# High and low parts of 109 weight units made by a rounding and an adding DMA on GpSimd's queue instead of ScalarE and VectorE

## The chip, the cores and the metric

The kernel runs on one core of a Trainium2 chip. The metric is the device time of one execution in microseconds. Before the change two runs gave 855.59 and 856.32 us, median 855.96 us.

The engines are called by their names in the profile: PE is TensorE's matrix multiplication and PEld its loading of weights, DVE is VectorE, ACT is ScalarE, POOL is GpSimd, SP is SyncE, which here only issues DMAs.

## The reference: what is computed

Two layers of a decoder trunk over 512 tokens of 1024 channels, in float32:

```python
for l in range(DEPTH):                                   # 2
    mod = c_act @ w_ada[l] + b_ada[l]
    shift, scale, gate = jnp.split(mod, 3, axis=-1)
    h = rms_norm(x, norm_g[l]) * (1.0 + scale[:, None, :]) + shift[:, None, :]
    u = h @ w_in[l]                                      # 1024 x 5120
    rg_x, rg_z, ml_x, ml_o, ml_z = jnp.split(u, split_pts, axis=-1)
    y_rg = rglru(causal_depthwise_conv(rg_x, ...), ...) * jax.nn.silu(rg_z)
    y_ml = mlstm_branch(ml_x, ml_o, ...) * jax.nn.silu(ml_z)
    y = jnp.concatenate([y_rg, y_ml], axis=-1) @ w_out[l]  # 2048 x 1024
    x = x + gate[:, None, :] * y
return rms_norm(x, final_g)
```

Most of the work lies in the two large products, `h @ w_in` and `y @ w_out`. The rest are the small block-diagonal products, the convolutions, the scan of the RG-LRU and the mLSTM's scores, gates and norms.

## The kernel before, in words

**Three products for one.** TensorE multiplies in the type `float32r`, which holds fewer bits than float32. To keep precision, every operand is split into a high part `hi`, the value rounded to float32r, and a low part `lo`, the rounded remainder, so that value = hi + lo nearly. `mm3` (L495) then issues three matrix multiplications for one: hi by hi, hi by lo and lo by hi.

**Weight units.** The weights are cut into units of 512 KB, tiles of 128 partitions by 1024 values. `load_raw` (L479) takes a tile of kind `raw` and has SP load it; `load_w` (L486) takes a tile `whi` and a tile `wlo` and splits the raw unit: ScalarE copies raw to hi (the copy rounds), VectorE subtracts hi from raw into lo. `split` (L464) is these two instructions. There are 3 raw slots, 4 slots `whi` and 4 slots `wlo` (L438 to L440). Three units of the front of layer 0, the first half of the rows of w_in for three groups of columns, are loaded and split in four pieces each (`pieces=4`, L1203).

The units go to these products, by the names that the profile uses for their output: `mx` (the mLSTM's input, `w_in_unit`, L724), `rgx` and `rgz` (through `chan_group`, L735), `oz` (the mLSTM's output gate and z, `ml_oz`, L959), `out` (first half of the output channels, `out_first`, L1116), and `outq` (third quarter in `out_quarter`, L1131; last quarter in `out_last`, L1146, whose four units are loaded at L1309 and held over four token blocks). Other loads stay with SP and with `split` or use raw tiles directly: `w_qk`, `w_vT`, `w_v`, `w_rg`, the adaLN weights `wada` and `w_ada2` (32 units through the raw slots, `mod_units`, L632), x, and small parameters.

**The stages of a layer.** The front computes shift, scale and h in five stages of channel blocks (layer 0: `STAGES`, L1190, with matrix products of the adaLN weights, `modps`, between them) and multiplies h with the first units of `mx`. Then come the per-head products (A, p, v, S), the gate chain (`gate_chain`, L906, with a power on GpSimd, the tile `u`), the four heads of oz with the mLSTM's tail (`num`, then `mrs`, a power on GpSimd, and the transposes `yT`), the RG-LRU half (rgx, gates, rgz, scan), and the output projection. In layer 0 the block norms of the next layer (`norm_x`, with `rstd`, a power on GpSimd) and the transposes `hT` start while the last quarter is still computed.

**What sets the order.** `Planner` (L108) records every instruction with a cost, its tiles and its engine, and then plans them all: `deadlines` (L243) goes backwards from TensorE's order and gives each instruction the latest time at which it must start, with 2.5 us on top for a DMA of SP; `schedule` (L286) plays the program forward, and at each moment an idle engine takes, of the instructions that are ready, the one with the earliest deadline. An engine doesn't idle if anything is ready. A tile gets a slot of its kind only if enough slots remain for tiles wanted earlier (`fits`, L313). The DMA engines are modelled as one server of 360 GB/s in order of issue, and a DMA of SP lands 2.0 us after that (L349 to L352). The result is a fixed order per engine, in which each engine works and waits on semaphores.

Of the kernel before, what the change touches and what calls it, by code (L numbers as in the profile page):

```python
# [13 lines left out]
F32R = mybir.dt.float32r  # L14
# [5 lines left out]
L = 2  # L20
# [10 lines left out]
# columns of the packed per-channel parameters  # L31
# [3 lines left out]
# what of adaLN is summed up on the vector engine: (layer, third)  # L35
# [3 lines left out]
# order of the rows of w_out: the mLSTM half first  # L39
CORD = list(range(8, 16)) + list(range(0, 8))  # L40
# where block j of the causal scores lies: (tile, first column)
# [4 lines left out]
class View:  # L46
    """A part of a logical tile; becomes an access pattern when its instruction is issued."""
# [60 lines left out]
class Planner:  # L108
    """Records instructions, then issues them on each engine in the order of a list schedule: the tensor
    engine follows the traced order, the others serve what it needs first."""  # L110
# [125 lines left out]

    def lat(self, a, b):
        if a != b:
            return self.LAT
        return 0.13 if a in ("DVE", "ACT", "POOL") else 0.0  # L240

# [1 line left out]
    def deadlines(self):  # L243
# [14 lines left out]
        # a PSUM bank is wanted again by a later tile; ready a little ahead of that  # L258
# [13 lines left out]
        for o in reversed(ops):  # L272
            d = o.pos
            for j in o.succ:
                s = ops[j]
                lat = self.lat(o.eng, s.eng)
                if o.eng == "SP":
                    lat += 2.5
                d = min(d, s.late - lat - o.cost)
            if o.eng != "PE":  # L280
                for b in o.tiles:
                    if b in after:
                        d = min(d, ops[after[b]].pos - o.cost)
            o.late = -100.0 if o.first else d

    def schedule(self):  # L286
# [4 lines left out]
        ready = {e: [] for e in engines}     # (late, i)  # L291
        events = []                          # (time, i): a finished instruction
        nfree = {k: [(0.0, s) for s in range(n)] for k, (n, _) in self.kinds.items()}
        # tiles still without a slot, by the deadline of their first use
# [18 lines left out]
        def fits(o):  # L313
            need = {}
            for b in o.tiles:
                if b.kind in self.kinds and b.slot is None:
                    need.setdefault(b.kind, []).append(b)
            for k, bs in need.items():
                room = len(nfree[k]) - len(bs)
                if room < 0:  # L320
                    return False
                # slots stay for the tiles that come before these
                ahead, w, h, last = 0, want[k], head[k], max(b.first for b in bs)
                while h < len(w) and w[h][0] < last:
                    if w[h][1].slot is None and w[h][1] not in bs:
                        ahead += 1
                        if ahead > room:
                            return False
                    h += 1
            return True  # L330

        def bank_free(o):
            # engines take turns at a PSUM bank
            return max((b.busy[1] for b in o.tiles if b.kind == "ps" and b.busy[0] != o.eng), default=0.0)

        def start(o, now):
# [12 lines left out]
            if o.eng == "SP":  # L349
                s = max(end, dma_free)  # L350
                dma_free = s + o.tail / 360e3
                end = dma_free + 2.0  # L352
# [5 lines left out]
        while done < len(ops):  # L358
# [23 lines left out]
            # next time at which something changes  # L382
# [43 lines left out]
def trunk_kernel(ctx: ExitStack, tc: tile.TileContext, x, cT, params, bif, bgate, fg,  # L426
# [6 lines left out]
    def pools(name, n, **kw):  # L433
# [5 lines left out]
        "whi": pools("whi", 4),  # L439
        "wlo": pools("wlo", 4),  # L440
# [53 lines left out]

    def mm3(ps, lh, ll, rh, rl, start, stop):  # L495
# [11 lines left out]
    # t < s: above any maximum, so that its exponential is 0; elsewhere below any  # L507
# [3 lines left out]
    # rows 32 q of four row groups; and pairs of groups, or all, row by row  # L511
# [42 lines left out]
    def log1p_exp_neg(ab, shape):  # L554
        # log(1 + exp(-ab)) for ab >= 0: u = exp(-ab), 2 atanh(u / (2 + u))
# [23 lines left out]
    # 4 softplus(-lambda), and halves of the biases of the RG-LRU gates, for both layers  # L579
# [18 lines left out]
    def mod_first(d0, nd):  # L598
        # shift and scale of the first layer, channel blocks d0 .. d0 + nd
# [5 lines left out]
        for k in range(4):  # L605
            # quadrants: (which, half of the rows)
# [25 lines left out]
    def mod_units(l, w):  # L632
        # third w (shift, scale, gate) of layer l: products and sums over the blocks of rows, one step a block
# [11 lines left out]
    def mod_sum(l, w):  # L645
        # the sum over the rows of a block
# [56 lines left out]
    def h_part(l, hT, xn, d0, nd, half):  # L703
        # channel blocks d0 .. d0 + nd of two token blocks, transposed, scaled, shifted, split
# [19 lines left out]
    def w_in_unit(l, g, kh, pieces=1):  # L724
        return load_w(w_in[l, g, kh], (4, 256), None, pieces)
# [27 lines left out]
    def silu2(ps, name, shape=(128, 512)):  # L753
        # 2 silu
# [15 lines left out]
    def fold(ps, sel, n):  # L770
        # rows 32 q + g of ps, transposed and summed over the groups q that sel joins: [128, chunk, n]
# [9 lines left out]
    def qk_weights(l, p, st):  # L781
        # A = w_q w_k^T, and the gates' weights seen through w_q and w_k
# [29 lines left out]
    def v_weights(l, u, st):  # L812
        # w_v of two heads, with the gates' columns beside it
# [24 lines left out]
    def ml_head(l, p, st):  # L838
# [34 lines left out]
        # scores, transposed, times 16; the gates' columns follow the last token  # L873
# [32 lines left out]
    def gate_chain(l, st):  # L906
# [13 lines left out]
        # sums of log f inside the blocks, and the blocks' totals on every partition  # L920
# [4 lines left out]
        # a[i - j][:, j]: log i - b of block j, from where block i starts  # L925
# [33 lines left out]
    def ml_oz(l, h, hT, st):  # L959
        # tanh(o / 2) and 2 silu(z) of a head, in two steps  # L960
        ps = [bank("oz") for _ in range(NB)]
        for u in range(4):
            wh, wl = load_w(w_oz[l, h, u], (2, 512))
# [16 lines left out]
    def ml_sw(h, st):  # L980
        # S * exp(a_s - M_t), causal, split
# [76 lines left out]
    def rg_gates(l, g, st):  # L1058
# [4 lines left out]
        for cc in range(2):  # L1063
# [6 lines left out]
            # r2 = 2 sigmoid(p) = (1 + |tanh(p / 2)|) exp(min(p, 0)); s = -log a = 4 sp r2;  # L1070
            # 1 - a^2 = tanh(s) (1 + a^2)
# [36 lines left out]
    def out_evac(l, ps, xt, cs):  # L1108
        # x + gate * y
# [6 lines left out]
    def out_first(l, st, xt, side):  # L1116
        y = st["y"]
        ps = [bank("out") for _ in range(NB)]
        for u in range(8):
            wh, wl = load_w(w_out[l, u], (2, 512))  # L1120
# [10 lines left out]
    def out_quarter(l, st, xt, side):  # L1131
        y = st["y"]
        ps = [bank("outq", (128, 256)) for b in range(NB)]
        for u in range(4):
            wh, wl = load_w(w_out[l, 8 + u], (4, 256))
# [20 lines left out]
    def final_pre(xt):  # L1156
        # of the first 768 channels: squares summed, x times the final gain
# [34 lines left out]
    for l in range(L):  # L1192
# [14 lines left out]
        if l == 0:  # L1207
            def front(n):
                # a stage's shift and scale, then its part of h, between the products of the stage before
# [99 lines left out]
        units = [load_w(w_out[l, 12 + u], (4, 256)) for u in range(4)]  # L1309
# [20 lines left out]
def _pack(inp):  # L1330
# [5 lines left out]
    def chan(v):  # [L, n * 128] -> [L, 128, n]  # L1336
# [7 lines left out]
    # adaLN, first layer's shift and scale: [channel block, k', p, quadrant, 128]; quadrant = (which, half of the rows)  # L1344
    wa = a["w_ada"].reshape(L, 2, 4, 128, 3, 8, 128)[0, :, :, :, 0:2]  # kh, k', p, which, block, n
    wa = wa.transpose(4, 1, 2, 3, 0, 5)  # block, k', p, which, half, n
# [4 lines left out]
    # o and z of a head side by side  # L1351
    oz = a["w_in"][:, :, 3072:].reshape(L, 4, 2, 128, 2, 4, 256)  # l, k pair, k, p, which, head, n
    w_oz = oz.transpose(0, 5, 1, 3, 2, 4, 6).reshape(L, 4, 4, 128, 1024)
    # transposed heads: l, h, m, e, d
# [7 lines left out]
    rg = np.stack([a["rg_w_a"], a["rg_w_x"]], axis=2)  # l, h, m, d, e  # L1362
# [32 lines left out]
```

## Time and profile before

| | |
|---|---|
| median of the runs | 855.96 us (855.59 to 856.32) |
| span of the profiled execution, first to last instruction | 853.5 us |
| granted TensorE clock, mean | 0.998 of full speed |
| DMA bytes moved | 107.60 MB, mean 126 GB/s |

The page gives no other time of the profiled execution than its span; 855.96 - 853.5 = 2.5 us lie around it, taken with the median of the runs.

How to read the profile. A group's row gives the source line, the engine, the operation, the output and input tiles with their shapes, the count, the busy time in us and the mean in ns, then the idle time of the engine just before the group's instructions and what ended it. In the view of waits a row says which engine and tile waited for which, the sum, the count and the longest. The chain is followed back from the last instruction, at each step to what released it. In the view of windows each row gives the stretch, its length, the busy time of PE, PEld, DVE, ACT and POOL with their counts, the granted clock, the share of the DMA engines' time and the GB/s. In the view of one tile, durations are minimum, median and maximum in ns. In the timeline a row starts with the start and the duration in us; SPq is the issue of a DMA by SP. Matrix multiplications are pipelined, so the durations of single ones overlap, and the chain shows their real pace.

### The profile page before, as it was taken

To read this page: it belongs to the slowest core of one execution; us is meant where nothing else is said; L and a number is where in the kernel's file an instruction comes from. 1 tells how busy PE (TensorE), PEld (TensorE's weight loads), DVE (VectorE), ACT (ScalarE), POOL (GpSimd) and SP (SyncE) were. 2 spreads that over 40 slices of the span, in tenths; PEclk is the share of its full clock that TensorE was granted. 3 is DMA by queue.
4 is the path that set the end of the run, shared out by engine and by line. 5 is a ranking of instruction groups with operands and counts; after the bars stand their busy time and mean duration, and the time that the engine had idled before them with its cause. 6 is when DMAs were issued, how large, how long until landed. Compare 5 with 4: busy or idle time off the path is not lost.

```text
span 853.5 us, 12548 instructions
## 1 busy us (share of the span) xinstructions
PE 835.0 (98%) x4664; PEld 698.1 (82%) x4664; DVE 607.3 (71%) x1227; ACT 476.7 (56%) x938; POOL 40.9 (5%) x66
## 2 busy tenths in 40 slices
PE   4999999999999999999999999999999999999996
PEld 3677897888888888887999789878888888888896
DVE  5467976898889699654466897376775877967643
ACT  4357763655457969622146766364454696893322
POOL 3000001011100000000010000100000000000000
PEclk9999999999999999999999999999999999999999
DMA  9924132466553323523231422033333222273202
GB/s 323 323 81 137 62 121 78 149 202 210 183 195 111 112 74 125 196 99 123 88 107 62 159 87 99 26 111 136 125 109 122 91 77 96 70 252 123 74 26 99
DMA packets 37053, 107.60 MB, mean 126 GB/s; under 512 B 4352, under 2 KB 6400, under 8 KB 36992
## 3 DMA queue, kind: packets, MB, share of 16 engines
q1 hardware_dynamic: 36992, 106.80, 36.2%
q8 instruction: 37, 0.61, 0.3%
q14 instruction: 24, 0.20, 0.1%
HBM read 102.58 MB, written 4.19 MB: 125 GB/s over the span
## 4 chain that ended last, share of the span: by engine, by line
PE 97%; DVE 1%; DMA 1%; POOL 1%; SPq 0%; ACT 0%; issue 0%; POOLq 0%
PE oz L153 20%; PE mx L153 11%; PE outq L153 11%; PE out L153 11%; PE rgz L153 10%; PE rgx L153 10%; PE S L153 4%; PE num L153 3%; PE v L153 3%; PE p L153 3%; PE A L153 2%; PE modps L153 2%; PE px L153 1%; PE pa L153 1%; PE hT L162 1%; PE yT L162 1%
## 5 line engine op out<-in xcount | busy, mean ns | idle before, releaser
L183 ACT CAST whi<-raw 128x1024 fp32r<-128x1024 f32 (+1 forms) x133 | 130.9, 994 | 186.7 <-PE oz L153 63.1
L190 DVE TENSOR_TENSOR wlo<-raw,whi 128x1024 fp32r<-128x1024 f32 (+1 forms) x133 | 151.9, 1148 | 72.4 <-ACT whi L183 72.0
L153 PE MATMUL oz<-whi,hh 128*128 128x512 f32 x256 | 101.8, 399 | 0.0
L153 PE MATMUL oz<-whi,hl 128*128 128x512 f32 x256 | 101.2, 395 | 0.0
L153 PE MATMUL oz<-wlo,hh 128*128 128x512 f32 x256 | 101.1, 395 | 0.0
L153 PE MATMUL outq<-whi,yh 128*128 128x256 f32 x256 | 72.5, 283 | 0.0
L153 PE MATMUL outq<-wlo,yh 128*128 128x256 f32 x256 | 72.4, 283 | 0.0
L153 PE MATMUL outq<-whi,yl 128*128 128x256 f32 x256 | 72.4, 283 | 0.0
L153 PE MATMUL mx<-hh,whi 128*128 128x512 f32 (+1 forms) x166 | 59.1, 358 | 0.0
L153 PE MATMUL mx<-hl,whi 128*128 128x512 f32 (+1 forms) x166 | 58.4, 352 | 0.0
L153 PE MATMUL mx<-hh,wlo 128*128 128x512 f32 (+1 forms) x166 | 57.4, 348 | 0.0
L153 PEld LDWEIGHTS oz<-whi,hh 128*128 128x128 f32 x256 | 48.1, 188 | 11.2 <-issue 1.0
L153 PEld LDWEIGHTS oz<-whi,hl 128*128 128x128 f32 x256 | 48.1, 188 | 11.1
L153 PEld LDWEIGHTS oz<-wlo,hh 128*128 128x128 f32 x256 | 48.1, 188 | 10.2
L153 PE MATMUL out<-whi,yh 128*128 128x512 f32 x128 | 50.6, 396 | 0.0
L153 PE MATMUL out<-whi,yl 128*128 128x512 f32 x128 | 50.6, 395 | 0.0
L153 PE MATMUL rgx<-hh,whi 128*128 128x512 f32 x128 | 50.5, 395 | 0.0
L153 PE MATMUL out<-wlo,yh 128*128 128x512 f32 x128 | 50.5, 394 | 0.0
L153 PE MATMUL rgz<-hh,whi 128*128 128x512 f32 x128 | 50.4, 394 | 0.0
L153 PE MATMUL rgz<-hl,whi 128*128 128x512 f32 x128 | 50.4, 394 | 0.0
L153 PE MATMUL rgx<-hl,whi 128*128 128x512 f32 x128 | 50.4, 394 | 0.0
L153 PE MATMUL rgz<-hh,wlo 128*128 128x512 f32 x128 | 50.4, 394 | 0.0
(256 smaller groups left out, 2029.7 us busy)
## 6 DMA issues: line engine op xcount, KB each, us to landing
raw<-in_w_in_dram SPq DMA_DIRECT2D x45, 512.0 KB, 3.2
raw<-in_w_oz_dram SPq DMA_DIRECT2D x32, 512.0 KB, 3.2
raw<-in_w_ada_dram SPq DMA_DIRECT2D x32, 512.0 KB, 3.3
raw<-in_w_out_dram SPq DMA_DIRECT2D x32, 512.0 KB, 3.2
wada<-in_w_adb_dram SPq DMA_DIRECT2D x24, 256.0 KB, 5.2
x<-in_x_dram SPq DMA_DIRECT2D x16, 256.0 KB, 5.5
raw<-in_w_qk_dram SPq DMA_DIRECT2D x8, 512.0 KB, 3.2
wada<-in_w_ada_dram SPq DMA_DIRECT2D x8, 256.0 KB, 4.3
```

The source lines that it names most:

```text
L153: self.nc.tensor.matmul(out.ap(), lhsT=lhsT.ap(), rhs=rhs.ap(), start=start, stop=stop, **kw)
L162: self.op("PE", lambda: self.nc.tensor.transpose(out.ap(), in_.ap(), ident.ap()), [out], [in_, ident], 0.109)
L183: self.op("ACT", lambda: self.nc.scalar.copy(out.ap(), in_.ap()), [out], [in_], 0.1 + 0.00084 * in_.n)
L190: self.op(eng, lambda: e.tensor_tensor(out=out.ap(), in0=a.ap(), in1=b.ap(), op=op), [out], [a, b], c)
```

## The change

For 109 units (45 of w_in in the front, rgx, rgz and mx, 32 of w_oz, 32 of w_out) a new function `dma_w` takes the place of `load_w`. It uses no raw tile. A DMA of GpSimd's queue loads the unit from memory straight into `hi`; since the destination's type is float32r, the transfer rounds. ScalarE writes minus hi into `lo`. A second DMA of GpSimd's queue reads the same unit from memory again and adds it to `lo`, so that lo = value - hi. The three units of the front that are loaded in pieces, and the units of w_qk, w_v and w_rg, keep `load_w`.

The planner learns the new DMA: 1.0 us of GpSimd for each, landing 3.0 us after the modelled transfer, and 4.5 us on top in the deadlines. The slots `whi` and `wlo` go from 4 to 5 each. The raw slots stay at 3. The rest of the diff removes comments.

```diff
+    def qdma(self, out, in_, nbytes, add=False):
+
+        def emit():
+            kw = {"accum_op": ALU.add} if add else {}
+            self.nc.gpsimd.dma_start(out.ap(), in_, **kw)
+
+        self.op("POOL", emit, [out], [out] if add else [], 1.0, tail=nbytes)
...
                 if o.eng == "SP":
                     lat += 2.5
+                elif o.tail:
+                    lat += 4.5
...
-            if o.eng == "SP":
+            if o.eng == "SP" or o.tail:
                 s = max(end, dma_free)
                 dma_free = s + o.tail / 360e3
-                end = dma_free + 2.0
+                end = dma_free + (2.0 if o.eng == "SP" else 3.0)
...
-        "whi": pools("whi", 4),
-        "wlo": pools("wlo", 4),
+        "whi": pools("whi", 5),
+        "wlo": pools("wlo", 5),
...
+    def dma_w(src, shape):
+
+        hi = P.tile("whi", (128,) + shape, F32R, "whi")
+        lo = P.tile("wlo", (128,) + shape, F32R, "wlo")
+        P.qdma(hi, shaped(src, shape), 1 << 19)
+        P.act(lo, hi.f32(), AF.Copy, scale=-1.0)
+        P.qdma(lo, shaped(src, shape), 1 << 19, add=True)
+        return hi, lo
...
     def w_in_unit(l, g, kh, pieces=1):
-        return load_w(w_in[l, g, kh], (4, 256), None, pieces)
+        if pieces > 1:
+            return load_w(w_in[l, g, kh], (4, 256), None, pieces)
+        return dma_w(w_in[l, g, kh], (4, 256))
...
-            wh, wl = load_w(w_oz[l, h, u], (2, 512))
+            wh, wl = dma_w(w_oz[l, h, u], (2, 512))
...
-            wh, wl = load_w(w_out[l, u], (2, 512))
+            wh, wl = dma_w(w_out[l, u], (2, 512))
...
-            wh, wl = load_w(w_out[l, 8 + u], (4, 256))
+            wh, wl = dma_w(w_out[l, 8 + u], (4, 256))
...
-        units = [load_w(w_out[l, 12 + u], (4, 256)) for u in range(4)]
+        units = [dma_w(w_out[l, 12 + u], (4, 256)) for u in range(4)]
```

## Prediction

> **What bounds the kernel now.** I read the page's head first, then TensorE's waits, then the chain that ended last.
>
> ```profile
> span 853.5 us, 12548 instructions
> ...
> PE 835.0 (98%) x4664; PEld 698.1 (82%) x4664; DVE 607.3 (71%) x1227; ACT 476.7 (56%) x938; POOL 40.9 (5%) x66
> ...
> q1 hardware_dynamic: 36992, 106.80, 36.2%
> ```
>
> TensorE is idle for 853.5 - 835.0 = 18.5 us in all. VectorE, ScalarE and the DMA engines have room on the average. What TensorE waited for:
>
> ```profile
> PE modps L153 <- DVE hb L206: 4.5, 1, 4.5
> PE modps L153 <- DMA wada<-in_w_ada_dram: 3.8, 1, 3.8
> PE hT L162 <- DVE xn L206: 2.4, 1, 2.4
> PE cumb L153 <- DVE lf L198: 1.1, 1, 1.1
> ```
>
> That is 11.8 us, and no weight unit is among it. The rest is the tail. The chain puts a price on one unit:
>
> ```profile
> by line: PE oz L153 20.2%; PE mx L153 11.0%; PE outq L153 10.7%; PE out L153 10.5%; PE rgz L153 10.4%; PE rgx L153 10.4%; PE S L153 3.5%; PE num L153 3.4%; PE v L153 2.8%; PE p L153 2.7%; PE A L153 1.7%; PE modps L153 1.6%; PE px L153 1.3%;
> ```
>
> The 32 units of oz take 0.202 x 853.5 = 172.4 us, 5.39 us each; the 16 of outq 91.3 us, 5.7 each. So TensorE eats one unit in about 5.4 us and bounds the kernel. A faster supply gains nothing, a later one costs its lateness.
>
> **What is removed.** 109 of the splits lose a ScalarE cast and a VectorE subtraction.
>
> ```profile
> L183 ACT CAST whi<-raw x133: 392/1050/1106, 14.2 to 824.5; 128x1024 fp32r<-128x1024 f32 x121, 128x256 fp32r<-128x256 f32 x12
> L190 DVE TENSOR_TENSOR wlo<-raw,whi x133: 412/1219/1246, 15.0 to 825.6; 128x1024 fp32r<-128x1024 f32 x121, 128x256 fp32r<-128x256 f32 x12
> L231 SPq DMA_DIRECT2D raw<-in_w_oz_dram x32: 327/328/383, 86.1 to 611.2; - x32
> ```
>
> VectorE gives back 109 x 1.219 = 133 us (607 to about 474). ScalarE exchanges a 1.05 us cast for a negation of the same shape: nothing. SP loses 109 issues of 0.33 us. All of it lies beside TensorE: 0 us of time.
>
> **What is added: two issues on GpSimd per unit.** No row shows a DMA issued there. From below the bound is SP's 0.33 us, from above GpSimd's dearest kind of instruction:
>
> ```profile
> L190 POOL TENSOR_TENSOR u<-ec,ng 128x16 f32<-128x16 f32 x3 | 9.8, 3269 | 30.6 <-DVE ng L206 30.6
> ```
>
> I take 1.0 us, what the changed planner books for one: nearer to SP's row, which is an issue too, than to the power, which computes element by element. Two make 2.0 us of each 5.4. It decides from 2.7 us per issue: at 3.27 GpSimd needs 6.5 us a unit.
>
> **The transfers.** q1's row gives 0.362 x 853.5 = 309 us for 106.8 MB, so 512 KB hold all 16 engines for 1.52 us. The rounding transfer replaces the old load at that price. The adding one is new. From below it costs 1.52; it has to read the source and the tile for one write, so two reads make 3.04, and a read, a second read and a write one after the other 4.56. I take 3.04. A unit then needs 4.56 us of DMA in 5.4, and the share of the DMA engines goes from 36% to 36.2 + 109 x 3.04 / 853.5 = 75%.
>
> In the Trainium skill, "Collectives: The Full Stack", section "The bandwidth ceiling", the adding primitive runs at half the copy's rate because it reads two sources, not because the add costs cycles. By that rule the sum below stays at 17 us; by 1.52 us it would be about 8. No run here shows it yet.
>
> **Latency of a unit.**
>
> ```profile
> raw<-in_w_oz_dram SPq DMA_DIRECT2D x32, 512.0 KB, 3.2
> ```
>
> Issue to landing is 3.2 us from SP, so 1.0 + 2.9 = 3.9 from GpSimd and 5.4 for the adding one. With the negation (1.05) and some 0.5 for hand-overs, 10.9 us pass from a free slot to a finished pair; before it was 1.05 + 1.22 once raw lay there. With five pairs of slots, four units of 5.4 us lie ahead, 21.6 us. That hides 10.9 in every steady stage: 0 us, as long as a unit costs neither DMA nor GpSimd more than 5.4 us. I see four places with less cover.
>
> **Place 1, the head.**
>
> ```profile
> 0.00:21.00 21.00, 10.24 (x92) 7.84 (x93) 12.01 (x58) 8.88 (x23) 8.34 (x22) 1.00 0.92 322
> 21.00:43.00 22.00, 22.00 (x157) 15.27 (x156) 9.80 (x35) 7.35 (x19) 0.00 (x0) 1.00 0.93 322
> 171.00:213.00 42.00, 42.00 (x205) 34.35 (x205) 38.67 (x91) 22.03 (x52) 4.88 (x4) 1.00 0.62 206
> 213.00:256.00 43.00, 43.00 (x221) 36.31 (x220) 35.23 (x81) 21.12 (x42) 2.88 (x3) 1.00 0.56 190
> ```
>
> The second column from the right is the DMA share: 0.92 and 0.93 up to 43 us, full. The split of the piecewise units follows its loads closely:
>
> ```profile
> 25.57 2.84 SPq L231 DMA_DIRECT2D raw<-in_w_in_dram  x5
> ...
> 31.87 1.94 ACT L183 CAST whi<-raw 128x256 fp32r<-128x256 f32 x6
> ...
> 36.77 2.13 SPq L231 DMA_DIRECT2D raw<-in_w_in_dram  x3
> ```
>
> SP loads the three second-half units of the front at 36.77, last. GpSimd, which computes only the norms' powers after its constants, is free from 2.7 us on:
>
> ```profile
> 2.63 0.11 POOL L575 MEMSET ec<- 128x16 f32 x1
> ```
>
> Of the five slot pairs three are kept for the piecewise units, so two second-half units start at once and their adding transfers some 8 us later. They bring 2 x (1.52 + 3.04) = 9.1 us of DMA work (6.1 if adding costs 1.52) ahead of x, adaLN weights and pieces, in a stretch with no room. About 1 us of slack lies between the pieces' landing and their use; the loads that fall away at 36.77 come too late to help. I take 9.1 - 1 = 8 us, bounds 0 (the engines serve SP's queue first) to 9. What is late next is the shift and scale of each stage, and TensorE's first products.
>
> **Place 2, the change of layers.**
>
> ```profile
> 442.52 5.13 PE mx L153 x43
> 447.64 1.31 PE hT L162 x12
> ```
>
> ```profile
> 434.89 1.05 ACT L183 CAST whi<-raw 128x1024 fp32r<-128x1024 f32 x1 [4.91 <-issue]
> ...
> 444.70 1.79 POOL L190 TENSOR_TENSOR rstd<-ms,mhalf 128x1 f32<-128x1 f32 x1 [4.04 <-DVE ms L206]
> ```
>
> out_last holds four pairs until its last block, so of layer 1's four front units one is ready and three start at about 434.9, 437 and 439. The first is ready at 434.9 + 10.9 = 445.8 and wanted at 442.52 + half of 5.13 = 445.1; the third ends after three units of DMA, 434.9 + 1.0 + 3 x 4.56 and a landing of some 2, about 452, and is wanted two quarters of p = 1 after the transposes, 448.95 + 2.6 = 451.6. Six issues also stand in GpSimd's order around the last norm's power (444.70), behind which VectorE and the transposes at 447.64 wait: 1 to 2 us. I take 3, bounds 0 to 8.
>
> **Place 3, the last quarter.** Its fourth unit gets the slot that out_quarter's third frees, 5.7 + 3/4 x 5.7 = 10.0 us ahead of its use, against 10.9: 1 us per layer, 2 in all, bounds 0 to 8.
>
> **Place 4, layer 0's oz.** The chain's rows at 184.13 and 211.42 are the same half of two heads, 27.3 us apart, with four units between them; num and yT belong to the mLSTM's tail, and the last row, from the timeline, to its powers on GpSimd:
>
> ```profile
> 184.13 11.12 PE oz L153 x48
> 195.25 3.60 PE num L153 x30
> ...
> 210.40 1.02 PE yT L162 x8
> 211.42 11.15 PE oz L153 x48
> ```
>
> ```profile
> 202.00 2.34 POOL L190 TENSOR_TENSOR mrs<-mms,mhalf 128x2 f32<-128x2 f32 x2 [24.06 <-DVE mms L206]
> ```
>
> From 171 to 256 us (rows above) the DMA is busy for 42 x 0.62 + 43 x 0.56 = 50.1 us of 85. Adding brings 85 / 27.3 x 4 x 3.04 = 37.9: 88.0 in 85. I take 3, bounds 0 (at 1.52) to 22 (at 4.56: 106.9 of 85).
>
> **New waits.** GpSimd works in order. A rounding issue waits for TensorE to free the slots, an adding one for the negation, and behind both stand the powers (mrs, rstd, u) and the memsets of vh. The mrs pair ends at 204.3, the transposes that need its result start at 210.4: one or two issues of 1.0 us between fit, 0 us. ScalarE in turn waits in order for the rounding transfer ahead of its negation, and evacuations stand behind it; with transfers as slow as taken the planner's own 1.0 + 1.5 + 3.0 us covers the wait, 0 us, and at twice that it belongs to the rate case. The gate chain's power (3.27 us, GpSimd) stands behind one issue more: 1 us, bounds 0 to 3, TensorE's 1.1 us wait on lf showing no cover.
>
> **Sum:** 8 + 3 + 2 + 3 + 1 = 17 us. The span becomes 853.5 + 17 = 870.5. Around it lie 856.0 - 853.5 = 2.5 us by the median of the runs, so the time is 873, and with the upper bounds of the head, the places 2 and 3 and the power 856 + 9 + 8 + 8 + 3 + 3 = 887.
>
> **Rivals.**
>
> *Hidden, not slower: 856.* GpSimd's early transfers are served behind SP's, the adding costs 1.52 us, and the places have their 10.9 us: one mechanism, a cover that holds everywhere; it decides if issue plus landing of both transfers stay under about 9 us. For it: no wait names a weight unit, and the DMA averages 36%. Against it: the full DMA of the head. Range 852 to 860.
>
> *Rate bound.* One engine needs more than 5.4 us a unit all along. GpSimd at 3.27 per issue: (6.54 - 5.4) x 109 = 124, with the 17 above 997. The adding transfer at 4.56: (6.08 - 5.4) x 109 = 74, with 17 above 947. For it: no row prices either; against it: 75% at my values. Decided from 2.7 us per issue, or 3.9 per adding transfer.
>
> *VectorE's copies stop GpSimd.* Descriptors that GpSimd writes could be held up by VectorE's copies:
>
> ```profile
> L213 DVE CAST hh<-hval 128x256 fp32r<-128x256 f32 x32 | 8.6, 289 | 7.7 <-ACT hval L176 7.6
> L206 DVE TENSOR_SCALAR xn<-x,rstd 128x512 f32<-128x512 f32 x16 | 7.9, 532 | 2.2 <-POOL rstd L190 1.7 <-POOL vh L860 0.4
> ```
>
> They last 16.5 us together and stand in the head and at the change of layers, where GpSimd is on the path: at most 873 + 16 = 889. The Trainium skill, "SBUF — State Buffer", section "SBUF: two separate sides", describes this as a trap of GpSimd's DMAs; no run here shows it.
> *Faster.* VectorE's relief could shorten the waits on hb, xn and lf, 4.5 + 2.4 + 1.1 = 8.0 us: 848 at best, 0.9%, and hb and xn lie before any split.
>
> **How the numbers follow.** Cover partly broken 0.47 (range 862 to 887, split about evenly by 873.1); hidden 0.23; rate bound 0.22; VectorE's copies 0.05; faster 0.03. The forecast is the likeliest, 873, slower than before. Two per cent, 17 us, is about what a measurement of this kernel can tell from no change: below 838.8 I see 0.02, above 873.1 0.24 + 0.22 + 0.05 = 0.51, and 0.47 between. The range goes down into the hidden case, to 853, and up into the rate-bound case, to 940.
>
> **What would show it.** Right: TensorE's busy time stays near 835 and its idle time grows by some 17 us; new waits on DMA wada, whi or wlo stand before 50 us and at 440 to 455; VectorE near 474 us; DMA share near 75%. Wrong in size: landing of the adding transfer under 4 us or over 7; GpSimd's issues over 2.7 us apart. Wrong altogether: TensorE waits for wlo evenly in oz, rgx and out (rate bound), or waits only as before (hidden).

## The result and the profile after

The changed kernel takes 870.56 us (868.86 and 872.25) against 855.96 us before: a ratio of 1.0173, 95% interval 1.0153 to 1.0194, slower by 14.6 us. That is just under the two per cent that the prediction took for the least a measurement can tell from no change, but the interval lies wholly above 1. The forecast was 873.

The head of the page of the changed kernel, and its two large DMA queues (packets, MB, share of 16 engines' span):

```profile
span 867.1 us, 12610 instructions
...
PE 835.7 (96%) x4664; PEld 698.1 (81%) x4664; DVE 489.3 (56%) x1118; ACT 473.2 (55%) x938; POOL 192.8 (22%) x284
...
q0 software_dynamic: 31392, 114.31, 58.4%
q1 hardware_dynamic: 21296, 49.64, 16.2%
```

TensorE is as busy as before (835.7 against 835.0 us) and idle for 31.4 us instead of 18.5. The two queues fill 74.6% of the DMA engines' time, where q1 alone had 36.2%. TensorE's idle time grew by 12.9 us, and the span by 13.6.

What TensorE waited for, in the changed kernel (sum, times, longest):

```profile
PE modps L153 <- DMA wada<-in_w_ada_dram: 11.2, 2, 5.9
PE hT L162 <- DVE xn L206: 2.6, 1, 2.6
PE mx L153 <- DMA wlo<-in_w_in_dram: 2.5, 1, 2.5
PE wqg L153 <- issue: 1.3, 2, 0.8
PE outq L153 <- DMA wlo<-in_w_out_dram: 1.0, 2, 0.6
```

Only 3.5 us of that (mx and outq) is a wait for a weight unit of the new kind, and mx has its wait at the change of layers, from 455.28 to 457.80 us. No row names oz, rgx, rgz or out. The wait on lf is gone.

Where the time went is read best by comparing the start of each product with that of the same product before. Worked out from the two traces, in us:

```
product of before starts at    late in the changed kernel
 26.7  modps                    +3.05
 51.7  mx                       +3.18
101.4  v                        +4.79
150.1  oz, layer 0              +4.84
400.5  outq, layer 0            +5.09
425.2  outq, last quarter       +6.83
444.0  mx, layer 1              +6.54
450.6  mx, layer 1             +12.36
475.3  mx, layer 1             +10.10
550.0  oz, layer 1              +9.98
575.3  oz, layer 1              +8.99
801.7  outq, layer 1            +8.84
846.8  last product             +9.08
end of the span                +13.6
```

Around 50 and around 450 us the changed kernel has some products in another order, so a single row there can stand above or below the loss (+12.36 at 450.6 us, +10.10 where the order is the same again). So 4.8 us are lost in the head, 0.3 from 101 to 400 us, 1.5 in layer 0's last quarter, 3.5 at the change of layers, 1.0 comes back in layer 1's gate chain, and 4.4 go after the last product.

The windows of the changed kernel (us, PE, PEld, DVE, ACT, POOL with counts, clock, DMA share, GB/s):

```profile
0.00:21.00 21.00, 7.14 (x51) 4.67 (x52) 11.05 (x55) 9.76 (x24) 10.48 (x23) 1.00 0.93 324
21.00:43.00 22.00, 21.68 (x178) 14.71 (x178) 9.99 (x35) 7.18 (x17) 1.72 (x5) 1.00 1.01 295
...
171.00:213.00 42.00, 42.00 (x215) 35.10 (x214) 30.00 (x82) 19.35 (x44) 10.97 (x14) 1.00 1.02 311
213.00:256.00 43.00, 43.00 (x216) 35.63 (x215) 29.23 (x72) 22.89 (x45) 12.26 (x17) 1.00 0.97 270
...
427.00:470.00 43.00, 39.02 (x320) 37.92 (x319) 17.77 (x59) 15.13 (x29) 10.39 (x18) 0.96 0.63 147
...
455.00:460.00 5.00, 2.48 (x18) 2.20 (x11) 4.06 (x15) 3.22 (x6) 0.85 (x1) 0.75 1.08 217
```

Layer 0's oz (171 to 256 us) has the DMA engines at 1.02 and 0.97, full, and TensorE idle for nothing. The head has TensorE busy for 7.14 us up to 21 us, where it had 10.24 before. The change of layers lacks 3.98 us. There the granted clock falls as well, to 0.75 in the last row: from 457.5 to 460.9 us the trace grants TensorE half its clock, and 13 products of mx start 0.21 us apart where their neighbours start 0.12 apart, some 1.3 us beside the wait of 2.5.

### The profile page after: what moved, and what is told of

It is laid out like the page before. It is cut to its first block, busy times and chain, and to the rows that moved or that the text cites. A ratio compares the mean times of both kernels' runs of the same rounds, so it can differ in the third digit from the quotient of the medians.

```text
span 867.1 us, 12610 instructions
## 1 busy us (share of the span) xinstructions
PE 835.7 (96%) x4664; PEld 698.1 (81%) x4664; DVE 489.3 (56%) x1118; ACT 473.2 (55%) x938; POOL 192.8 (22%) x284
## 3 DMA queue, kind: packets, MB, share of 16 engines
q1 hardware_dynamic: 21296, 49.64, 16.2%
## 4 chain that ended last, share of the span: by engine, by line
PE 80%; issue 9%; DMA 3%; POOL 3%; DVE 2%; ACT 1%; SPq 1%; POOLq 0%; DVEq 0%
PE oz L153 21%; PE mx L153 10%; PE rgx L153 9%; PE rgz L153 8%; PE outq L153 7%; PE out L153 5%; PE S L153 3%; PE num L153 3%; PE v L153 3%; PE p L153 2%; PE A L153 2%; POOL wlo L241 1%; POOL whi L241 1%; DMA wlo<-in_w_in_dram 1%; PE modps L153 1%
## 5 line engine op out<-in xcount | busy, mean ns | idle before, releaser
L176 ACT ACTIVATE wlo<-whi 128x1024 fp32r<-128x1024 f32 x109 | 116.0, 1064 | 141.8 <-DMA whi<-in_w_out_dram 66.3
L241 POOL DMA_DIRECT2D wlo<-in_w_in_dram x45 | 39.3, 873 | 147.7 <-ACT wlo L176 111.9
L153 PEld LDWEIGHTS oz<-whi,hh 128*128 128x128 f32 x256 | 48.1, 188 | 10.9 <-issue 0.5
L198 DVE SCALAR_TENSOR_TENSOR macc<-raw,csil,macc 128x512 f32<-128x512 f32 x56 | 40.2, 747 | 22.7 <-DMA raw<-in_w_ada_dram 22.7
L241 POOL DMA_DIRECT2D whi<-in_w_in_dram x45 | 25.6, 568 | 123.3 <-PE rgx L153 35.1
L153 PE MATMUL rgx<-hh,wlo 128*128 128x512 f32 x128 | 50.4, 393 | 0.0
```

The lines of the kernel that those rows point to most:

```text
L153: self.nc.tensor.matmul(out.ap(), lhsT=lhsT.ap(), rhs=rhs.ap(), start=start, stop=stop, **kw)
L176: self.nc.scalar.activation(out=out.ap(), in_=in_.ap(), func=func, **kw)
L198: self.nc.vector.scalar_tensor_tensor(out=out.ap(), in0=a.ap(), scalar=sv, in1=b.ap(), op0=op0, op1=op1)
L241: self.nc.gpsimd.dma_start(out.ap(), in_, **kw)
```

## Experiments

The first theory: the steady stages hide the two transfers, and the loss stands at four places: the head, the last quarters, the change of layers and the end of the program. The rivals: the adding transfers' traffic costs time all along; or the software queue has a fixed price whatever it carries.

The kernel before ran beside each batch of experiments, with medians of 855.6 to 855.9 us.

### The end: one unit in the kernel before

From the start of the last product to the end of the span the kernel before needs 6.75 us and the changed one 11.19. The work there is the same. SP waits at its closing instructions longer. In the kernel before, from 845 us on:

```profile
SPq L1391 <- PEq L1391: 0.6, 2, 0.4
```

and in the changed one, from 855 us on:

```profile
SPq L1412 <- PEq L1412: 4.7, 2, 4.2
```

The row names PE's sequencer, which had been done long before. GpSimd's stream has a closing DRAIN instruction, which starts as its last power does; the trace's record of it lasts 0.636 us before the change and 8.292 us after (857.99 to 866.29). The closing instructions of all engines follow it. The first experiment makes one unit of the kernel before by the two transfers (with `qdma`, `dma_w` and the planner's lines of the change):

```diff
-            wh, wl = load_w(w_oz[l, h, u], (2, 512))
+            wh, wl = (dma_w if (l, h, u) == (1, 0, 2) else load_w)(w_oz[l, h, u], (2, 512))
```

> The kernel before with one of its units (layer 1, first head's third unit of oz) made by the rounding and the adding DMA, all else as before. Theory A, the end costs a fixed amount as soon as GpSimd has issued a DMA (its closing drain lasts 8.29 us instead of 0.64 after its last power, and the end of the program waits for it): the time grows by 4.4 us to 860.3, with TensorE's last product at 847.1 as before. Rival B, the drain grows with the number of transfers (218 of them cost 4.4 us): 856.0, no change.

Measured: 856.0 us, ratio 1.0005 (0.9995 to 1.0014), the drain 0.824 us. Theory A's fixed price falls, and B holds: two transfers lengthen it by 0.19 us only.

### The end: the last norm's root without GpSimd

```diff
-        P.tt(rstd, ss, mhalf[:, 0:1], ALU.pow, eng="POOL")
+        P.act(rstd, ss, AF.Sqrt)
+        P.recip(rstd, rstd)
```

> The changed kernel, where the last norms' reciprocal root is made by ScalarE (Sqrt) and VectorE (reciprocal) instead of GpSimd's power, so that GpSimd's last instruction is an adding issue near 835 us. Theory A, the drain starts after GpSimd's last instruction and takes 8.3 us: it ends under the last quarter and the end of the program shrinks from 10.9 us after the last product to 6.5, so 866.2. Rival B, the end waits 4 us more whatever GpSimd did last: 870.6.

Measured: 867.86 us (865.33 to 870.54), ratio 1.0145 (1.0119 to 1.017). From the start of the last product to the end 6.91 us pass, 4.3 fewer than in the changed kernel, as theory A has it. The drain is no shorter, 10.084 us, but it starts with the last adding issue at 836.25 us and lies under the last quarter. In the view of waits, from 855 us on, the row is back at

```profile
SPq L1413 <- PEq L1413: 0.7, 2, 0.5
```

The whole time fell by 2.7 us only, and A's 866.2 was missed. In the profiled execution the head, whose program is the same, came out longer: at 101 us it is 6.6 us late, not 4.8, with a wait of 12.3 us on wada.

The same edit was also made in the kernel before:

> The kernel before with the last norms' power replaced by ScalarE's square root and VectorE's reciprocal, and nothing else. Theory A (what this edit gains in the changed kernel is the hidden drain alone): the kernel before, whose drain is 0.64 us, gains nothing, 855.3 to 856.5 us, and the stretch from the last product to the end stays at 6.4 to 7.1 us. Rival B (the power on GpSimd is slow in itself there): 2 us or more faster, under 854 us.

Measured: 855.46 us, ratio 0.9999 (0.999 to 1.0009), and 6.56 us from the start of the last product to the end. The edit gains nothing where the drain is short. So the drain, and not the power, is what costs 4.4 us.

### The head: layer 0's second-half units back to SP

```diff
-        if pieces > 1:
+        if pieces > 1 or (l == 0 and 8 <= g <= 10):
             return load_w(w_in[l, g, kh], (4, 256), None, pieces)
```

> The changed kernel, but layer 0's three second-half units of the front go back to SP's load and the split by ScalarE and VectorE. Theory A, the 4.8 us that TensorE lost by 85 us come from these units (their transfers run ahead of x and the adaLN weights, their adding transfers come late): 870.6 - 4.8 = 865.8, with TensorE's products within 0.5 us of the kernel before from 85 us to 400 us. Rival B, the loss comes from the DMA load all along or from the new order of GpSimd: 869 to 871.

Measured: 865.74 us (864.12 to 868.08), ratio 1.0128 (1.0112 to 1.0145). That is A's time, but only half of it for A's reason. The products stand 0.6 us late from 23 to 55 us, not 3.1. But from 91 us on they stand 2.3 us late, with v waiting 1.2 us for the split of w_v: "within 0.5 us" missed. So the head gives back 2.5 us. Another 2.4 us come from the last quarter and the change of layers, where this execution loses 2.6 us and that of the changed kernel 5.0: mx waits about as long, 2.66 us, but no stretch at half clock follows. The drain is 7.808 us.

### The head: the same units, later

```diff
+HOLD = 20.0
...
             if o.ndep == 0:
-                heapq.heappush(ready[o.eng], (o.late, o.i))
...
+                if o.eng == "POOL" and o.tail:
+                    heapq.heappush(pending, (HOLD, o.i))
+                else:
+                    heapq.heappush(ready[o.eng], (o.late, o.i))
```

> The changed kernel, but no rounding transfer is issued in the plan before 20 us. Theory A, two early rounding transfers (2 x 1.52 us) push x and the adaLN weights back by the 3.1 us that TensorE's first products of mx are late: these are on time, and the time is 870.6 - 3.1 = 867.5 unless the units themselves then come late by 50 us. Rival B, the first products are late for another reason, the order of GpSimd's constants or norms: still 3 us late, 870.6.

Measured: 864.1 us (863.08 to 864.59), ratio 1.0099 (1.0084 to 1.0114). At 26.7 us the products are 1.8 us late, where A had them on time; 1.5 us of that is there by 16.02 us, ahead of the first transfer of GpSimd's queue at 17.32, so it is not these transfers' doing. At 51.7 us the product of the table stands 6.0 us late, since others now go ahead of it, but from 91 us on only 1.4: 3.4 us of the head's 4.8 are gone, close to A's 3.1. The other 1.5 us of the span's gain come at the change of layers (1.60 late at 400 us and 4.74 at 475, a loss of 3.1 where the changed kernel loses 5.0): mx waits 2.61 us there, and again no stretch at half clock follows. It is faster than the changed kernel, and not than the one before.

The timeline of GpSimd in the changed kernel tells what the early transfers are:

```profile
1.53 1.47 POOL L241 DMA_DIRECT2D whi<-in_w_in_dram  x2
...
19.16 0.93 POOL L241 DMA_DIRECT2D wlo<-in_w_in_dram  x1 [0.16 <-ACT whi L183]
...
35.49 0.87 POOL L241 DMA_DIRECT2D wlo<-in_w_in_dram  x1 [14.33 <-ACT whi L183]
...
58.55 0.86 POOL L241 DMA_DIRECT2D wlo<-in_w_in_dram  x1 [16.26 <-ACT wlo L176]
```

Two rounding transfers are issued from 1.53 us on, ahead of most of SP's loads of x and wada, and land at 7.80 and 9.62 us. Two times 1.52 us is 3.0, near the 3.05 us by which the first products are late. That the two agree so well is partly chance, since executions differ here: with the same early transfers the first products are 4.90 us late in the version with the root on ScalarE and 3.48 us in the one below that overwrites, and in the four versions with no such transfer ahead of 17 us they lie between 0.4 us early and 1.8 us late. The adding ones follow at 19.16 and 35.49 us only, since ScalarE's negation comes after more urgent work, and the third at 58.55 us. No product of the head waits for one of these units.

### The adding transfer: overwrite instead of add

```diff
-        P.qdma(lo, shaped(src, shape), 1 << 19, add=True)
+        P.qdma(lo, shaped(src, shape), 1 << 19)
```

> The changed kernel, but the second transfer of each unit overwrites lo with the rounded unit instead of adding to it (the low parts are wrong, so the output differs). Theory A, adding costs twice a rounding transfer (3.1 and 1.52 us of 16 engines, 4.65 us for the pair measured): the share of GpSimd's queue falls from 58.4% to about 38.5%, lo lands as hi does, in about 5 us instead of 7.2 to 7.8, and the places with little cover lose 2.5 us of latency each: 866 to 868. Rival B, each DMA of this queue costs 2.3 us because GpSimd writes its descriptors or because it rounds: the share stays near 58%, the time near 870.6.

Measured: 867.29 us (866.76 to 870.88), ratio 1.0143 (1.0125 to 1.016). Its queue and its landing times (KB, median us from issue to landing):

```profile
q0 software_dynamic: 31392, 114.31, 41.4%
...
whi<-in_w_oz_dram POOLq DMA_DIRECT2D x32, 512.0 KB, 3.8
wlo<-in_w_oz_dram POOLq DMA_DIRECT2D x32, 512.0 KB, 4.6
```

0.414 x 865.1 / 218 = 1.64 us for a plain transfer of 512 KB in this queue. In the changed kernel a pair takes 0.584 x 867.1 / 109 = 4.65 us, so the adding one takes 4.65 - 1.64 = 3.0 us. Of the 506 us in which the queue's transfers hold the DMA engines 148 were taken away, 29%, and 3.3 us of 14.6 came back (most of the gain at the last quarter and the change of layers, where 5.0 became 1.1, some 1.3 us of it the stretch at half clock, which this trace lacks), while the drain grew to 9.807 us. The traffic is not what costs the time in the steady stages: theory A.

### The rate: two rounding transfers per unit

```diff
         P.qdma(hi, shaped(src, shape), 1 << 19)
+        P.qdma(hi, shaped(src, shape), 1 << 19)
```

> The changed kernel with the rounding transfer of each unit made twice, one after the other (the same values). A unit then costs the 16 engines 1.52 + 1.52 + 3.1 = 6.2 us in the 5.4 that TensorE takes for it. Theory A, the steady stages are covered only as long as this stays under 5.4: now each of some 105 units is 0.8 us late, about 870.6 + 80 = 950, with TensorE waiting for wlo evenly in oz, rgx and out. Rival B, the cost of the change is latency at a few places: 3 to 8 us more, 874 to 879.

Measured: 907.0 us (904.48 to 910.06), ratio 1.0599 (1.0575 to 1.0623). Here a unit costs 0.721 x 906.9 / 109 = 6.0 us of DMA against the 5.4 in which TensorE eats it. The transfer that was put in thus adds 6.0 - 4.65 = 1.35 us, less than the 1.64 found above, so prices read from these shares hold to some 0.3 us, and the adding one lies between 3.0 and 3.3. TensorE's waits and the windows of this kernel:

```profile
PE oz L153 <- DMA wlo<-in_w_oz_dram: 10.6, 5, 3.4
PE out L153 <- DMA wlo<-in_w_out_dram: 9.5, 6, 7.1
PE rgx L153 <- DMA wlo<-in_w_in_dram: 7.0, 4, 2.2
```

```profile
171.00:256.00 85.00, 76.59 (x356) 62.08 (x357) 56.27 (x145) 35.57 (x79) 26.00 (x36) 0.96 1.06 332
256.00:341.00 85.00, 81.77 (x367) 66.03 (x366) 53.92 (x92) 61.41 (x95) 25.77 (x39) 1.00 0.92 241
```

That is what rate bound looks like: waits in every stage that eats units, and lateness that grows from 4.8 us at 150 to 52.7 at the end. About 10 us of this are not waits: TensorE is busy for 846.1 us instead of 835.7, with seven stretches at half clock ahead of the end, two of them in the row with 0.96. The change costs 36 us over the changed kernel and not the 80 that A gave. Where few units are taken nothing more is lost (the lateness stays at 32 us from 475 to 550 us), and the excess is 0.6 us a unit and not 0.8. The kind of A's answer was right, its size double.

### The cover: four slots instead of five

```diff
-        "whi": pools("whi", 5),
-        "wlo": pools("wlo", 5),
+        "whi": pools("whi", 4),
+        "wlo": pools("wlo", 4),
```

> The changed kernel with 4 slots of whi and wlo as before, instead of 5. A pair takes 4.8 + 1.1 + 7.4 + some 0.6 = 13.9 us from the free slot; three units ahead are 16.2. Theory A, steady stages stay covered and the places lose a slot: the last quarter's fourth unit has 4.3 us instead of 10 in both layers (+10 each, less the 1.5 of now), the change of layers has no unit ready (+5): 890, between 882 and 900. Rival B, the wait for a slot decides everywhere: more than 1 us for each unit, over 950.

Measured: 891.73 us (885.09 to 892.59), ratio 1.0402 (1.0371 to 1.0434). The time lies in A's range by luck, for the loss stands elsewhere than A put it. The last quarters lose 1.6 and 1.1 us and not 10 each, the change of layers about 6, and the stages rgz and out, which A held to be covered, 3.0 in layer 0 and 8.0 in layer 1. With one unit of 5.4 us less ahead, stages that hid everything begin to wait:

```profile
PE out L153 <- DMA wlo<-in_w_out_dram: 5.6, 3, 3.1
PE rgz L153 <- DMA wlo<-in_w_in_dram: 4.0, 2, 3.8
```

The fifth slot carries about 21 us of this change.

### The edges: fifteen units back, and the end without GpSimd

```diff
-        if pieces > 1:
+        if pieces > 1 or (l == 0 and 8 <= g <= 10) or (l == 1 and 8 <= g <= 9):
...
-        units = [dma_w(w_out[l, 12 + u], (4, 256)) for u in range(4)]
+        units = [load_w(w_out[l, 12 + u], (4, 256)) for u in range(4)]
...
-        P.tt(rstd, ss, mhalf[:, 0:1], ALU.pow, eng="POOL")
+        P.act(rstd, ss, AF.Sqrt)
+        P.recip(rstd, rstd)
```

> The changed kernel, but the units of the places go back to SP and split: layer 0's three units of the front, layer 1's four units of the front, the four units of each last quarter, 15 of 109; and the last norms' root is made without GpSimd. Theory A, the loss is head 4.8, change of layers 3.5, last quarter 1.5 and the closing drain 4.4, and VectorE's relief gives 1.1 back in layer 1's gate chain: all but about 1 us of head goes, 855 to 857, the same as before. Rival B, what is left of the 94 units still costs by its DMA load: 860 or more.

Measured: 856.71 us (856.43 to 858.17), ratio 1.0015 (1.0006 to 1.0024), as A. TensorE's waits are those of the kernel before without the one on lf, and one for w_v's split:

```profile
PE modps L153 <- DVE hb L206: 4.9, 1, 4.9
PE modps L153 <- DMA wada<-in_w_ada_dram: 4.3, 1, 4.3
PE hT L162 <- DVE xn L206: 2.4, 1, 2.4
PE v L153 <- DVE wvl L190: 1.2, 1, 1.2
```

94 of 109 units still come by the two transfers, with 50.9% of the DMA engines' time, and cost nothing from 101 us on: at 475 us the products are 2.2 us late, 2.4 at 101, and at the end 1.2. What stays lost is 1.5 us of the head between 70 and 85 us, where v waits for w_v's split. The last quarters and the change of layers were taken back together only, not one by one. GpSimd's drain still lasts 8.862 us here, but from 802.53 us on, under the products.

The next version is this one with the power left on GpSimd, without the last three lines of the edit:

> The 15 units at the edges (three of layer 0's front, four of layer 1's front, eight of the two last quarters) go back to SyncE's queue and the VectorE split, as in the run before this one of the same family, but the last norm's power stays on GpSimd. Theory A (GpSimd's closing drain is long after many software transfers and starts behind that power): 94 units keep the drain at 7 to 10 us, so the end costs 3.5 to 4.5 us more than with the root on ScalarE: 859.5 to 861.5 us. Rival B (the drain shrinks with the units left or costs nothing of its own): 856 to 857.5 us, a drain under 2 us.

Measured: 858.79 us (857.95 to 859.46), ratio 1.0036 (1.0022 to 1.005), a drain of 5.806 us and 8.75 us from the start of the last product to the end, against 6.99 with the root on ScalarE. That is A's direction, and under its range: the drain was shorter than 7 to 10 us.

### The gain in the gate chain: one unit of oz

Layer 1's gate chain gave 1.0 us back. In the kernel before, VectorE and GpSimd have these two rows, each from the timeline of its engine:

```profile
545.25 1.23 DVE L190 TENSOR_TENSOR wlo<-raw,whi 128x1024 fp32r<-128x1024 f32 x1
```

```profile
545.26 3.98 POOL L190 TENSOR_TENSOR u<-ec,ng 128x16 f32<-128x16 f32 x1 [15.98 <-DVE ng L206]
```

In the changed kernel the subtraction is gone and the same power is shorter:

```profile
555.23 2.93 POOL L190 TENSOR_TENSOR u<-ec,ng 128x16 f32<-128x16 f32 x1 [1.68 <-DVE ng L206]
```

Layer 0's power has such a subtraction beside it too (1.25 us long, in the kernel before), but one that starts at 132.84 us, 0.05 us after the power, and there the power is not longer:

```profile
132.79 2.90 POOL L190 TENSOR_TENSOR u<-ec,ng 128x16 f32<-128x16 f32 x1 [13.09 <-DVE ng L206]
```

```diff
+            wh, wl = (dma_w if (l, h, u) == (1, 1, 0) else load_w)(w_oz[l, h, u], (2, 512))
```

> The kernel before with one unit alone made by the two transfers: the first unit of oz of layer 1's second head, whose subtraction on VectorE (545.25 us, 1.23 us long) starts together with GpSimd's power of the gate chain (545.26 us, 3.98 us long, against 2.93 us in the changed kernel). Theory A (that subtraction held up the power, and the 1.1 us that the changed kernel gains in layer 1's gate chain come from this one pair): the power takes 2.9 to 3.0 us, TensorE no longer waits 1.1 us for lf, and the products after the gate chain start 0.9 to 1.1 us earlier than those of the kernel with another single unit exchanged; time 854.6 to 855.4 us. Rival B (the gain comes from VectorE's lighter load at large): the power stays near 4.0 us, the wait on lf at 1.1 us, 855.7 to 856.5 us.

Measured: 854.88 us, ratio 0.9993 (0.9984 to 1.0002). The power takes 2.93 us in its timeline, the wait on lf is gone from the list, and the products go from 0.49 us late before the gate chain to 0.55 early after it, a step of 1.04 us:

```profile
545.73 2.93 POOL L190 TENSOR_TENSOR u<-ec,ng 128x16 f32<-128x16 f32 x1 [1.47 <-DVE ng L206]
```

The time alone can't tell it from no change; the profile can, and it answers as A. Its median lies 0.8 us under that of the kernel before, and the interval includes no change.

## Why the prediction was right, and where its steps were not

The time was right within 3 us and the sum near (13.6 us of span against 17), and its mechanism was right for the most part: TensorE bounds, the steady stages hide the two transfers, and the loss stands where little cover is. But the sum's nearness is partly luck, from errors that cancel: places 1 and 4 were 6 us too dear and the gate chain 2, the end, 4.4 us, was missing, and 1.3 of the 3.5 us at the change of layers came from a fall of the clock that no step held.

**What bounds, and what the relief is worth.** TensorE's busy time stayed, and the subtractions that left VectorE (132.6 us by their rows, 118 of its busy time) brought nothing through VectorE's load; it is busy for 489.3 us, where 474 was forecast. "Faster" named lf as a place; there the gain came, for another reason than a lighter load: one subtraction that ran together with GpSimd's power.

**Two issues on GpSimd.** Taken at 1.0 us each. The groups of the changed kernel:

```profile
L241 POOL DMA_DIRECT2D wlo<-in_w_in_dram x45 | 39.3, 873 | 147.7 <-ACT wlo L176 111.9 <-ACT whi L183 14.5 <-PE wfT L153 7.5
...
L241 POOL DMA_DIRECT2D whi<-in_w_in_dram x45 | 25.6, 568 | 123.3 <-PE rgx L153 35.1 <-PE mx L153 24.7 <-PE rgz L153 22.7
```

0.57 us for the rounding one and 0.87 for the adding one, 1.44 per unit against 2.0: far from the 2.7 apiece that would decide.

**The transfers.** Adding at 3.04 us, by two reads for one write, measured 3.0 to 3.3; a pair at 4.56, measured 4.65; the DMA share at 75%, measured 74.6. The runs show the price; that two reads make it is not shown. The rule of the Trainium skill, "Collectives: The Full Stack", section "The bandwidth ceiling", that adding runs at half the copy's rate, agrees roughly: 3.0 against 1.64 us, or 3.3 against 1.35.

**Latency of a unit.** Taken at 10.9 us, with landings of 3.9 and 5.4. The DMA rows of the changed kernel:

```profile
whi<-in_w_oz_dram POOLq DMA_DIRECT2D x32, 512.0 KB, 4.5
wlo<-in_w_oz_dram POOLq DMA_DIRECT2D x32, 512.0 KB, 7.3
```

With the negation (1.06) and the same 0.5 that is 4.5 + 1.06 + 7.3 + 0.5 = 13.4 us. This step was too cheap: the adding transfer lands in 7.2 to 7.8 us by the medians, over the 7 that the prediction itself had named as a sign of a wrong size. The landings were priced from a kernel whose DMA engines are 36% busy, and these are three quarters busy. 21.6 us of units ahead cover 13.4 as well, and TensorE waits for no unit in a steady stage; with 16.2 us ahead (four slots) it does.

**Place 1, the head: 8 predicted, 4.8 measured.** The step that failed is "two second-half units start at once and their adding transfers some 8 us later". The rounding transfers did start at once and were served ahead of most of SP's loads. The adding ones waited for ScalarE until 19 and 35 us, when the first products had begun. Some 3 us of the 9.1 us of DMA work fell on the path (3.05 in this execution). The remaining 1.8 us came later, in waits that the prediction didn't name: 0.9 us for w_v's split at 83.44 us, 0.5 ahead of wqg at 58.80, 0.3 and 0.2 for an input of hT and of A. None of these is for a unit of the new kind, and why they came is not taken apart.

**Place 2, the change of layers: 3 predicted, 3.5 measured,** at the place that was named, but not by the same terms. From the chain of waits of the changed kernel, 425 to 470 us:

```profile
444.47 0.54 POOL whi L241
...
445.50 0.62 POOL rstd L190
...
446.91 0.57 POOL whi L241
...
448.32 0.52 POOL whi L241
448.84 8.92 DMA wlo<-in_w_in_dram
...
457.80 12.24 PE mx L153 x90
```

Issues do stand around the norms' powers, but no row has the transposes wait for them here, so the 1 to 2 us put on them did not come. What came is the wait for a unit, 2.5 us, and for the first that starts late: its rounding issue is at 441.66 us, its adding issue at 448.84, and it lands at 457.76, 16.1 us after the start where the prediction took 10.9. Less the 6.5 us of lateness that arrived, it is ready at 451.3, where 445.8 had been worked out. The stretch at half clock that follows adds some 1.3 us. It came in this execution and in that with the root on ScalarE, after waits of 2.5 and 2.7 us, and not in the two versions of the head's experiments, after 2.7 and 2.6 us. There the place costs 1.8 us. What decides it is not shown.

**Place 3, the last quarter: 1 per layer predicted;** 1.5 in layer 0, 0.1 in layer 1.

**Place 4, layer 0's oz: 3 predicted, 0 measured.** The 88.0 us of DMA work in 85 was nearly right (shares of 1.02 and 0.97 make 84.6). The step that failed was to put the excess of 3 us on the path, though the units ahead hold 21.6 us and a unit needs 13.4: an excess that ends before the lead is used up costs nothing.

**The gate chain: 1 lost predicted, 1.0 gained in layer 1.** No issue stood ahead of the power; what had stood beside it went away.

**Not in the sum: the end, 4.4 us.** The prediction put nothing on the stretch behind the last product, and gave no reason; GpSimd's closing drain stands there. The range of the forecast held it, but no step did.

**Rivals.** Hidden was right for the steady stages and wrong for the edges; the version with its edges taken back shows both, at 856.7 us. Rate bound didn't come, and one more transfer per unit shows how near it was: 6.0 us a unit where 5.4 are to be had. VectorE's copies: the 45 adding issues of w_in last 835 to 1045 ns, in the head as elsewhere, so no sign of a stop.

## What to carry to other kernels

Work that is taken from an engine that doesn't bound is worth nothing by itself, and a longer way to the same data is hidden only where enough units lie ahead: compare the latency with the lead at each edge (start, change of stage, held slots, end) and not with the average. When a second DMA queue is put to use early, count its transfers as served among the first's, not behind its backlog. Where a small instruction of GpSimd stands on the path, look in the timeline at what VectorE starts just ahead of it.

## What the runs showed of the hardware that was not expected

**GpSimd's closing drain.** Its length after so many transfers on GpSimd's queue, from the traces:

```
transfers   kernel                                drain, us
  0         before                                 0.636
  0         before, root on ScalarE                1.091, hidden
  2         one unit (two different ones)          0.824, 0.822
188         edges taken back, power on GpSimd      5.806
188         edges taken back, root on ScalarE      8.862, hidden
212         front back to SP                       7.808
218         changed; front later; four slots       8.292; 8.298; 8.256
218         overwriting instead of adding          9.807
218         changed, root on ScalarE               10.084, hidden
327         rounding twice                         4.540
```

"Hidden" stands where GpSimd's last instruction comes long before the end. Behind the last power the drain grows with the transfers up to 218, but 327 gave less and overwriting more, so their number alone doesn't set it. What does is left open. In the changed kernel some 4 us of it run beside the last output transfers (SP's own closing instruction stands at 862.17 us, the drain ends at 866.29), and the rest, 4.1 us, is most of what the end costs.

**A power that VectorE holds up.** The power on 128x16 values took 3.98 us when a VectorE subtraction of 1.23 us started 10 ns ahead of it, and 2.93 us without. The Trainium skill, "SBUF — State Buffer", section "SBUF: two separate sides", describes an exclusive port of the two engines that a VectorE instruction with two inputs there keeps from a GpSimd instruction that reads, and that goes to whichever starts first; the 1.05 us agree with it, and so does the power of layer 0, which started 0.05 us ahead of a subtraction and took 2.90 us.
